# A GDN layer's head work, issued at other steps of TensorE's order

## The chip, the cores and the metric

The kernel runs on one core of a Trainium2 chip. The metric is the device time of one execution in microseconds (us); lower is better. Five engines work from queues of their own: TensorE (PE; its weight loads are shown as PEld), VectorE (DVE), ScalarE (ACT), GpSimd (POOL) and SyncE (SP), which issues the transfers.

## The reference

A trunk of two layers over one sequence of 1024 positions with 1024 channels: a gated DeltaNet (GDN) layer and an mLSTM layer, each with a residual, and a last RMS norm. Only places in the GDN layer move. For each of its 8 heads (128 key channels, 256 value channels) it computes

```python
q, k, v = split(silu(causal_dwconv(h @ w_in)))          # per head; q and k are normalised
L    = exp(gc[i] - gc[j]) for j <= i, else 0              # decay inside a chunk
a    = I + strict_lower(beta * (k @ k.T) * L)             # per chunk
u    = solve(a, beta * v)                                 # unit lower triangular
wk   = solve(a, beta * exp(gc) * k)
attn = (q @ k.T) * L
for each chunk:                                           # S: 128 x 256, carried on
    w = u - wk @ S
    o = (q * exp(gc)) @ S + attn @ w
    S = exp(gc[-1]) * S + (k * exp(gc[-1] - gc)).T @ w
out  = (rmsnorm(o) * silu(z)) @ w_out
```

The kernel works with chunks of 128 positions (8 of them, in two halves of 4) and builds the inverse of `a` for each chunk from 32x32 blocks.

## The kernel before

**The projections.** `h @ w_in` is the bulk of TensorE's work. Each operand is held as a high and a low part, and each product is three matmuls of 128x512 (high by high, high by low, low by high; the names `hh`, `hl`, `_hi`, `_lo` in line L480). One `k` of a product, three matmuls, is a *step*. The steps of all projections of the layer run one after another, head by head; a head's window is 64 steps (head 0), 96 (head 1) or 88 (heads 2 to 7); work at a step past the end stands in the next head's window.

**The head's other work** is written as Python generators, each of which issues its instructions piece by piece. A table says for each generator at which steps of its head's window it goes on by one piece: first entry head 0, second head 1, third heads 2 to 7. On TensorE the order is exactly that of the program (`manual_schedule`), so a piece's matmuls stand in TensorE's queue where the table puts them. The other engines' orders are made by a scheduler from the same program, and each engine then works through its own queue in that order, waiting at whatever isn't ready.

```python
for n, _ in enumerate(steps_of(*(c.products() for c in cols), late())):
    for gen in plan.get(n, ()):
        do(gen)
```

The generators, with the names that rows show:

- **keys** (`KEYS`, `gdn_keys`): transposes of the keys (`tpk`, L849), their squares on ACT (L852), `kd` on DVE (L873), the decay row `growb` by DMA (L858), `at` (L878), products `kk` of keys with keys (L891), from which DVE makes `nt` (L894); `nt` goes to memory and comes back as `nd` (L900, L903).
- **queries** (`QUERIES`, `gdn_queries`): transposes `tpq` (L849), their squares on ACT (`sqrq`, L852) and `eq` on DVE (L914), products `kq` (L920), which DVE multiplies into `at` (L921).
- **solve**, the substitution (`SOLVE`, `gdn_solve`): 31 pairs of DVE instructions on `nd` (`pr` L940, `xr` or `xt` L942), each pair on the result of the one before, then a way through memory (`tb_dram` L947, `td` L950).
- **merge** (`MERGE`, `gdn_merge`, once a half): DVE puts `td` into `tt` and transposes it into `t` (L959, L962, L963); TensorE makes `xp` from `t` (L971), ACT and DVE copy it to `xs` (L977, L978), TensorE makes `yp`, which is copied back into `tt` (L982 to L984); then `xl`, `xls` and `yl` in the same way at width 64.
- **values** (`TOKENS`, `gdn_tokens`): transposes of the values (L838) and their copies.
- **scan** (`SCAN`, `gdn_scan`; its table stays): per chunk `ks` from the state S (L1018), `rr` on DVE (L1020), `y` from `rr` and `tt` (L1023), `w` on ACT (L1025), `sn`, S on DVE (L1030, L1035), `o`, its RMS factor `g_r` (ACT, DVE, POOL; L392 to L394), `gv_h` on ACT (L1043), and for the chunk before the output gate `go` (L356, L359) and a store `gg_dram` (L1006).
- **blocks** (`BLOCKS`, `first_blocks`): sums and differences of input blocks (`hs`, L455 to L458, and L438) for a product scheme used from head 2 on.

The scan of a head runs while the next head's projections are on TensorE, so that scan pieces of head h and keys, solve and merge of head h+1 stand between the same projection steps. PSUM tag `d` has two banks, which `tpk`, `kk`, `tpq`, `kq`, the value transposes, the gate and the merge's products take in turn.

Of the kernel before, what the change touches and what calls it, by code (L numbers as in the profile page):

```python
# [51 lines left out]
LASTENDS = ((4, 4), (6, 8), (8, 8))  # L52


KEYS = ((4, 9, 11, 14), (28, 31, 32, 35), (22, 25, 26, 29))
QUERIES = ((17, 20, 22, 30), (68, 71, 76, 76), (82, 82, 86, 91))
SOLVE = (27, 44, 32)
MERGE = ((78, 82), (86, 93), (86, 100))
TOKENS = ((37, 37, 81, 85), (71, 74, 97, 103), (64, 68, 107, 110))
SCAN = (91, 113, 102)  # L60
PACE = ((3, 3, 8), (4, 3, 10), (4, 3, 11))
BLOCKS = (101, 115, 114, 132)
XLOADS = (24, 116)
LAST = (156, 158, 157, 159)
TH = HT * P
# [3 lines left out]
def hybrid_kernel(ctx, tc, x_in, norm_w, final_norm_w, gdn_w_in, gdn_conv_w, gdn_a_log, gdn_dt_bias, gdn_norm_w,  # L69
# [394 lines left out]
    def last_block(temp, e):  # L464

        for k in range(4):
            a = temp(k)
            whole(V, a, blocks["A12"][k])
            add_parts(V, a, a, blocks["S2"][k], ALU.subtract)
            put("S4", k, a, e)  # L470
            yield
# [358 lines left out]
    def gdn_tokens(h, st):  # L830

        for half in range(2):
            v = hp.tile([P, HT, DV], F32, tag="v", bufs=2, name=f"gv{h}_h{half}")
            st["v"].append(v)
            for e in range(ET):
                vp = pwork(f"gvp{h}_{e}_{half}", "d")
                for c in range(HT):
                    nc.tensor.transpose(vp[:, c * P:(c + 1) * P], st["vt"][e, half][:, c * P:(c + 1) * P], ident)  # L838
                A.copy(v[:, :, e * P:(e + 1) * P], vp.rearrange("p (c d) -> p c d", c=HT))
                if e == ET - 1:  # L840
                    G.tensor_tensor(v, v, st["irk"][:, half * HT:half * HT + HT].unsqueeze(2).to_broadcast([P, HT, DV]),
                                    ALU.mult)
                yield
# [62 lines left out]
    def gdn_queries(h, st):  # L906

        sq, eq = (sp.tile([P, NT], F32, tag=n, name=f"{n}{h}") for n in ("sq", "eq"))
        st["eq"] = eq
        for half in range(2):  # L910
            hs = slice(half * HT, half * HT + HT)
            q, k, at = st["q"][half], st["k"][half], st["at"][half]
            squares_t(q, sq, "q", h, half)
            V.tensor_scalar(eq[:, hs], sq[:, hs], 1e-6, EPS * DK, ALU.add, ALU.mult)  # L914
            dec_b = decay_row(1, h, half)
            yield
            kq = pwork(f"kq{h}_{half}", "d").rearrange("p (c i) -> p c i", c=HT)
            for c in range(HT):
                s_ = slice(c * P, (c + 1) * P)
                mm(kq[:, c, :], k[:, s_], q[:, s_], start=True, stop=True)  # L920
            V.tensor_tensor(at, kq, at, ALU.mult)  # L921
            G.tensor_tensor(q, q, dec_b, ALU.mult)
            yield

    def gdn_solve(h, st):


        nd = st["nd"].rearrange("p (j i) -> p j i", i=BLK)
        rows = sp.tile([P, BLK // NG4 * BLK], F32, tag="t", bufs=2, name=f"xr{h}")
        nc.sync.dma_start(rows, unit_rows)  # L930
        xp = pwork(f"xt{h}", "x")[:, :BLK // NG4 * BLK] if h > 1 else rows
        xt = xp.rearrange("p (i r) -> p i r", r=BLK)
        if h > 1:
            A.copy(xp, rows)
        yield
        for j in range(BLK - 1):
            m, n = j // NG4 + 1, BLK - 1 - j
            pr = sp.tile([P, m, n], F32, tag="td", bufs=1, name=f"pr{h}_{j}")
            with behind() if j == 0 else nullcontext():
                V.tensor_tensor(pr, xt[:, :m, j:j + 1].to_broadcast([P, m, n]),  # L940
                                nd[:, j:j + 1, j + 1:].to_broadcast([P, m, n]), ALU.mult)
            st["solved"] = V.tensor_tensor(xt[:, :m, j + 1:], xt[:, :m, j + 1:], pr, ALU.add)  # L942
            yield
        st["tb"] = dp.tile([NG4, NT, NB, BLK // NG4, BLK], F32, tag="tb", bufs=2, name=f"tb_dram{h}")
        if h > 1:
            A.copy(rows, xp)
        nc.sync.dma_start(st["tb"].rearrange("g c b i r -> (g c b) (i r)"), rows)  # L947
        st["td"] = tds = sp.tile([P, NT, BLK], F32, tag="td", bufs=1, name=f"td{h}")
        for g in range(NG4):
            nc.sync.dma_start(tds[g::NG4], st["tb"][g].rearrange("c b i r -> (b i) c r"))  # L950
        yield
# [118 lines left out]
    with tc.manual_schedule(engines={mybir.EngineType.PE}):  # L1070
# [26 lines left out]
        def at_steps(steps, gen):  # L1097
            for step in steps:
                plan.setdefault(step, []).append(gen)
# [15 lines left out]
        for h, (st, base) in enumerate(zip(sts, starts)):  # L1115
            i = min(h, 2)
            off = lambda steps: [base + n for n in steps]
            for half in range(2):
                at_steps(off(range(MERGE[i][half] - 4, MERGE[i][half] + 16, 4)), gdn_merge(h, st, half))
            at_steps(off(KEYS[i]), gdn_keys(h, st, range(2)))  # L1120
            at_steps(off(QUERIES[i]), gdn_queries(h, st))
            at_steps(off(SOLVE[i] + n // 2 for n in range(BLK + 1)), gdn_solve(h, st))
            at_steps(off(TOKENS[i]), gdn_tokens(h, st))
        temps = lambda k: [wp.tile([P, TH], F32, tag="wraw", bufs=WB, name=f"hs{k}_{i}") for i in range(2)]

        def first_blocks():
            gen = h_blocks(temps, (G, V, G))
            for k in range(4):
                with tc.issue_after(sts[0]["merged" if k else "solved"].ins):
                    next(gen)  # L1130
                yield

        at_steps(BLOCKS, first_blocks())
        at_steps(LAST, last_block(lambda k: temps(k)[0], V))
# [491 lines left out]
```

## Time and profile before

| what | value |
|---|---|
| median of 3 runs | 1971.52 us (1967.94 to 1972.74) |
| the profiled execution | 1967.29 us, its span 1965.6 us |
| TensorE busy | 1886.7 us, 96% of the span |
| DVE, ACT, POOL busy | 1271.1, 1006.8, 692.7 us |
| mean granted clock of TensorE | 0.993 |

The span is what the trace covers; the rest of the execution lies around it. A granted clock of 1.00 is TensorE at its full clock of 2.4 GHz and 0.50 at its lower level of 1.2 GHz; a number in between is a stretch with both. A row of the timeline gives start, duration, engine, line, operation, result and operands, and in brackets the time that the engine stood idle just before, with what it waited for.

### The profile page before, as it was taken

How to read it: one execution, taken by the hardware profiler on the slowest of the kernel's cores; microseconds unless marked ns; L12 is line 12 of the kernel's file. 1: busy time of each engine (PE TensorE's matmuls, PEld its weight loads, DVE VectorE, ACT ScalarE, POOL GpSimd, SP SyncE). 2: the span in 40 equal slices, each digit the busy share in tenths (PEclk: the TensorE clock that was granted, in tenths of full speed). 3: DMA queues.
4: the chain of work that ended last, by engine and by line, in shares of the span. 5: the costliest groups of instructions: out<-in, count | busy, mean ns of one | idle time of the engine just before them, and what ended most of it. 6: DMA issues, size and time to landing. Idle time of an engine off the chain costs nothing.

```text
span 1965.6 us, 28818 instructions
## 1 busy us (share of the span) xinstructions
PE 1886.7 (96%) x9768; PEld 1550.2 (79%) x9768; DVE 1271.1 (65%) x2877; ACT 1006.8 (51%) x2325; POOL 692.7 (35%) x621
## 2 busy tenths in 40 slices
PE   5998999999999999999999999999999999999987
PEld 3786787878787878787888788888888888878876
DVE  6678686858595959547555866666666666673313
ACT  5536454646465555545445554545554645564423
POOL 4234334333333334100121333333433333355553
PEclk9999999999999999999999999999999999999999
DMA  4211122121222222636421221212121221246332
GB/s 141 87 42 49 54 71 78 58 75 57 79 63 67 65 67 77 197 109 232 122 86 56 78 74 59 73 57 82 61 80 63 70 68 65 81 137 205 105 119 76
DMA packets 138620, 171.24 MB, mean 87 GB/s; under 512 B 30860, under 2 KB 68584, under 8 KB 138472
## 3 DMA queue, kind: packets, MB, share of 16 engines
q1 hardware_dynamic: 138472, 169.40, 27.5%
q8 instruction: 77, 1.26, 0.3%
q14 instruction: 71, 0.58, 0.1%
HBM read 142.87 MB, written 26.48 MB: 86 GB/s over the span
## 4 chain that ended last, share of the span: by engine, by line
PE 77%; DVE 10%; DMA 4%; ACT 3%; issue 2%; POOL 1%; SPq 1%; DVEq 0%; ACTq 0%; POOLq 0%
PE lout L679 8%; PE gkv_ps L480 7%; PE gout L679 7%; PE mkq_ps L480 7%; PE mv_ps L480 7%; PE mz_ps L480 6%; PE mog_ps L480 6%; PE gqv_ps L480 5%; PE gzp_ps L480 4%; PE mo L1455 1%; PE mv_ps L1212 1%; PE gv_ps L480 1%; PE o L1040 1%; PE y L1023 1%; PE out L384 1%
## 5 line engine op out<-in xcount | busy, mean ns | idle before, releaser
L394 POOL TENSOR_TENSOR g_r<-g_r,mhalf 128x1 f32<-128x1 f32 x64 | 41.4, 647 | 212.5 <-DVE g_r L393 192.4
L268 DVE SCALAR_TENSOR_TENSOR gw_lo<-gw_raw,rest,gw_hi 128x256 fp32r<-128x256 f32 x128 | 61.3, 516 | 66.0 <-ACT gw_hi L267 66.0
L263 POOL TENSOR_TENSOR lw_lo<-lw_raw,lw_hi 128x512 fp32r<-128x512 f32 x56 | 72.9, 1304 | 73.4 <-ACT lw_hi L262 69.9
L679 PE MATMUL lout<-lgp_hh,lw_hi 128*128 128x512 f32 x224 | 88.7, 396 | 4.6 <-DVE y L1414 3.2
L263 POOL TENSOR_TENSOR mog_lo<-mog_raw,mog_hi 128x512 fp32r<-128x512 f32 x39 | 50.3, 1290 | 115.3 <-ACT mog_hi L262 115.3
L263 POOL TENSOR_TENSOR mz_lo<-mz_raw,mz_hi 128x512 fp32r<-128x512 f32 x39 | 53.8, 1379 | 99.7 <-ACT mz_hi L262 99.7
L267 ACT ACTIVATE gw_hi<-gw_raw,rest 128x256 fp32r<-128x256 f32 x128 | 58.0, 501 | 58.3 <-PE gout L679 42.3
L679 PE MATMUL lout<-lgp_hl,lw_hi 128*128 128x512 f32 x224 | 87.7, 392 | 0.0
L679 PE MATMUL lout<-lgp_hh,lw_lo 128*128 128x512 f32 x224 | 86.8, 392 | 0.0
L263 POOL TENSOR_TENSOR mv_lo<-mv_raw,mv_hi 128x512 fp32r<-128x512 f32 x38 | 51.4, 1353 | 84.1 <-ACT mv_hi L262 53.1
L263 POOL TENSOR_TENSOR gkv_lo<-gkv_raw,gkv_hi 128x512 fp32r<-128x512 f32 x40 | 52.8, 1322 | 78.3 <-ACT gkv_hi L262 67.8
L480 PE MATMUL gkv_ps<-hh,gkv_hi 128*128 128x512 f32 x176 | 78.9, 448 | 0.0
L263 POOL TENSOR_TENSOR gzp_lo<-gzp_raw,gzp_hi 128x512 fp32r<-128x512 f32 x38 | 49.7, 1307 | 66.8 <-ACT gzp_hi L262 55.4
L262 ACT CAST lw_hi<-lw_raw 128x512 fp32r<-128x512 f32 x56 | 34.7, 620 | 73.7 <-PE lout L679 48.9
L263 POOL TENSOR_TENSOR mkq_lo<-mkq_raw,mkq_hi 128x512 fp32r<-128x512 f32 x35 | 45.6, 1302 | 75.9 <-ACT mkq_hi L262 64.8
L480 PE MATMUL gkv_ps<-hh,gkv_lo 128*128 128x512 f32 x176 | 69.2, 393 | 0.0
L480 PE MATMUL gkv_ps<-hl,gkv_hi 128*128 128x512 f32 x176 | 69.0, 392 | 0.0
L679 PE MATMUL gout<-glp_hh,gw_hi 128*128 128x512 f32 x160 | 66.7, 417 | 0.0
L394 POOL TENSOR_TENSOR m_r<-m_r,mhalf 128x1 f32<-128x1 f32 x64 | 42.6, 665 | 66.2 <-DVE m_r L393 65.2
L679 PE MATMUL gout<-glp_hl,gw_hi 128*128 128x512 f32 x160 | 62.7, 392 | 0.0
L679 PE MATMUL gout<-glp_hh,gw_lo 128*128 128x512 f32 x160 | 62.7, 392 | 0.0
L1043 ACT ACTIVATE gv_h<-o,g_r 128x256 f32<-128x256 f32 x64 | 30.3, 473 | 62.5 <-POOL g_r L394 61.8
(769 smaller groups left out, 6688.0 us busy)
## 6 DMA issues: line engine op xcount, KB each, us to landing
gw_raw<-in_gdn_w_out_dram SPq DMA_DIRECT2D x64, 256.0 KB, 2.7
lw_raw<-in_mlstm_w_out_dram SPq DMA_DIRECT2D x56, 256.0 KB, 2.7
gzp_raw<-in_gdn_w_in_dram SPq DMA_DIRECT2D x32, 256.0 KB, 3.2
growb<-g_dram SPq DMA_DIRECT2D x32, 256.0 KB, 3.2
gg_dram<-gv_h SPq DMA_DIRECT2D x64, 128.0 KB, 1.8
gl<-gg_dram SPq DMA_DIRECT2D x32, 256.0 KB, 3.4
mog_raw<-in_mlstm_w_in_dram SPq DMA_DIRECT2D x32, 256.0 KB, 3.1
mz_raw<-in_mlstm_w_in_dram SPq DMA_DIRECT2D x32, 256.0 KB, 2.9
```

The costliest lines, as they stand in the source:

```text
L262: A.copy(hi, raw)
L263: (e or G).tensor_tensor(lo, raw, hi.bitcast(F32), ALU.subtract)
L267: A.activation(hi[:, k], raw[:, k], AF.Copy, scale=c)
L268: V.scalar_tensor_tensor(lo[:, k], raw[:, k], c, hi.bitcast(F32)[:, k], ALU.mult, ALU.subtract)
L384: mm(ps, a[:, e, ds], b[:, e, hs], start=m == 0, stop=m == 3 * ET - 1)
L394: G.tensor_tensor(r, r, mhalf[:, :1], ALU.pow)
L480: mm(ps, w_[:, k, :], h_, start=first and k == 0 and i == 0, stop=k == 3 and i == 2, skip_group_check=True)
L679: mm(pss[2 * j + i], a[:, e, i * P:(i + 1) * P], b, start=h == heads[0] and e == 0 and m == 0, stop=h == heads[-1] and e == ET - 1 and m == 2)
L1023: mm(yp[:, :DV], st["tt"][half][:, cc, :], rr, start=True, stop=True)
L1040: mm(op[:, :DV], st["at"][half][:, cc, :], w, start=S is None, stop=True)
L1043: A.activation(v, op[:, :DV], AF.Copy, scale=r)
L1212: mm(ps[c], h_[k][half][:, c * P:(c + 1) * P], w_[:, k % 2, :], start=k == 0 and i == 0, stop=k == KT - 1 and i == 2)
```

## The change

Places in the tables move; no instruction is added or taken away, and no shape changes.

```diff
-KEYS = ((4, 9, 11, 14), (28, 31, 32, 35), (22, 25, 26, 29))
-QUERIES = ((17, 20, 22, 30), (68, 71, 76, 76), (82, 82, 86, 91))
-SOLVE = (27, 44, 32)
-MERGE = ((78, 82), (86, 93), (86, 100))
-TOKENS = ((37, 37, 81, 85), (71, 74, 97, 103), (64, 68, 107, 110))
+KEYS = ((2, 7, 8, 15), (32, 35, 36, 39), (22, 25, 26, 29))
+QUERIES = ((17, 20, 23, 30), (68, 71, 76, 76), (80, 80, 84, 89))
+SOLVE = (24, 44, 32)
+MERGE = ((78, 82), (86, 89), (88, 100))
+TOKENS = ((37, 37, 81, 85), (71, 74, 97, 103), (64, 74, 107, 110))
...
-BLOCKS = (101, 115, 114, 132)
+BLOCKS = (101, 115, 114, 126)
```

Head 0's keys and substitution go up to three steps earlier, head 1's keys four steps later, head 1's second merge half four steps earlier, and the blocks' last piece six steps earlier. For heads 2 to 7 (one table entry, so the same places six times) the queries go two steps earlier, the first half of the merge two steps later and the second piece of the values six steps later. What that makes of the queues is shown at three places.

TensorE's queue in the late part of head 5's window. `hh_6_1` is the activation of k = 6, second half of the positions; `xp_0`, `yp_0` are the merge of head 5, first half; `tpq_1`, `kq_1` its queries, second half; `ks_7`, `y_7` the scan of head 4, last chunk; `gzp` and `gkv` are projections. Before:

```order
L480 MATMUL gzp_ps_6232<-hh_6_1_435,gzp_4_lo 128x512
L971 MATMUL xp_0_6342<-t_0_6278,nt_0_5652 32x32 x8
L849 MATMUL tpq_1_6354<-ident,gqT_1_6091 128x128 x4
L480 MATMUL gzp_ps_6232<-hh_7_1_440,gzp_4_hi 128x512
...
L1018 MATMUL ks_7_6372<-S_6_6313,gkT_1_4472 128x256
L480 MATMUL gkv_ps_6376<-hh_0_0_233,gkv_00_hi 128x512
...
L971 MATMUL yp_0_6392<-xs_0_6351,tt_0_6277 32x32
...
L1023 MATMUL y_7_6411<-rr_7_6374,tt_1_5434 128x256
L920 MATMUL kq_1_6415<-gqT_1_6091,gkT_1_5500 128x128 x4
```

And after:

```order
L849 MATMUL tpq_1_6336<-ident,gqT_1_6091 128x128 x4
...
L480 MATMUL gzp_ps_6232<-hh_7_1_440,gzp_4_lo 128x512
L1018 MATMUL ks_7_6360<-S_6_6308,gkT_1_4472 128x256
L480 MATMUL gkv_ps_6364<-hh_0_0_233,gkv_00_hi 128x512
...
L971 MATMUL xp_0_6374<-t_0_6332,nt_0_5652 32x32 x8
...
L920 MATMUL kq_1_6389<-gqT_1_6091,gkT_1_5500 128x128 x4
...
L1023 MATMUL y_7_6402<-rr_7_6362,tt_1_5434 128x256
...
L971 MATMUL yp_0_6409<-xs_0_6383,tt_0_6331 32x32
```

`xp_0` has moved behind `tpq_1`, the three matmuls of k = 7, `ks_7` and the next product's first three matmuls; `kq_1` now stands ahead of `y_7`, and `yp_0` behind it.

DVE's queue at the same place (`t_0`, `xs_0`, `tt_0` belong to the merge, `rr_7` to the scan, `eq` to the queries, `gzp_u` and `gkv_raw` to the projections). Before:

```order
L962 STREAM_TRANSPOSE t_0_6278<-tt_0_6277 64x256
L525 TENSOR_TENSOR gkv_raw_6028<-gkv_raw_6028,gkv_raw_6025 128x512
L978 COPY xs_0_6351<-xp_0_6342 32x128
L614 TENSOR_TENSOR gzp_u_6098<-gzp_u_6098,gzp_ps_6232 128x512
L1020 SCALAR_TENSOR_TENSOR rr_7_6374<-ks_7_6372,nlam,gv_h_5554 128x256
L963 STREAM_TRANSPOSE t_1_6463<-td_5992 32x4x32
L914 TENSOR_SCALAR eq_6283<-sq_6282 128x4
L983 COPY tt_0_6277<-yp_0_6392 32x4x32
```

And after:

```order
L962 STREAM_TRANSPOSE t_0_6332<-tt_0_6331 64x256
L525 TENSOR_TENSOR gkv_raw_6028<-gkv_raw_6028,gkv_raw_6025 128x512
L914 TENSOR_SCALAR eq_6272<-sq_6271 128x4
L614 TENSOR_TENSOR gzp_u_6098<-gzp_u_6098,gzp_ps_6232 128x512
L1020 SCALAR_TENSOR_TENSOR rr_7_6362<-ks_7_6360,nlam,gv_h_5554 128x256
L963 STREAM_TRANSPOSE t_1_6463<-td_5992 32x4x32
L978 COPY xs_0_6383<-xp_0_6374 32x128
L921 TENSOR_TENSOR at_1_5682<-kq_1_6389,at_1_5682 128x512
```

The copy `xs_0` has gone behind `rr_7`, and `eq` ahead of it.

SP's queue in head 1's window (`growb` the decay rows, `nt_dram` and `nd` the way of the keys' `nt` through memory, `gg_dram` the scan's store, `gzp_raw` and `gkv_raw` loads of weights). Before:

```order
L490 DMA gzp_raw_1283<-in_gdn_w_in_dram 128x512 x2
L858 DMA growb_0_2003<-g_dram 128x512
L900 DMA nt_dram_0_1498<-nt_0_1493 32x4x32 x4
L903 DMA nd_1428<-nt_dram_0_1498 16x1024 x4
L900 DMA nt_dram_1_1567<-nt_1_1562 32x4x32 x4
L1006 DMA gg_dram<-gv_h_1027 128x2x128
L903 DMA nd_1428<-nt_dram_1_1567 16x1024 x4
L490 DMA gkv_raw_1718<-in_gdn_w_in_dram 128x512 x2
```

And after:

```order
L490 DMA gzp_raw_1283<-in_gdn_w_in_dram 128x512 x2
L858 DMA growb_1_1547<-g_dram 128x512
L858 DMA growb_0_2020<-g_dram 128x512
L900 DMA nt_dram_0_1524<-nt_0_1519 32x4x32 x4
L1006 DMA gg_dram<-gv_h_1045 128x2x128
L903 DMA nd_1475<-nt_dram_0_1524 16x1024 x4
L490 DMA gkv_raw_1718<-in_gdn_w_in_dram 128x512
L900 DMA nt_dram_1_1614<-nt_1_1609 32x4x32 x4
L490 DMA gkv_raw_1718<-in_gdn_w_in_dram 128x512
L903 DMA nd_1475<-nt_dram_1_1614 16x1024 x4
```

The transfers of `nt` to memory and of `nd` back now stand between the store and two loads of weights, and a load stands ahead of each of the last two.

On TensorE head 1's keys stand like this: `tpk_0`, `kk_0`, `tpk_1` and `kk_1` were behind the first-chunk scan's `sn_0` (ahead of it for `tpk_0`), `o_0`, `ks_1` and `y_1`; now `tpk_0` is behind `ks_1`, `kk_0` behind `y_1`, `tpk_1` three matmuls after it, and `kk_1` behind `go_0`. In head 0, `tpk_0` now stands right behind `gr_ps` (L783), ahead of six projection matmuls that stood between.

## Rows read from the trace of the kernel before

**Rows 1.** The page's first part: engine, busy us, share of the span, instructions.

```profile
PE 1886.7 (96%) x9768; PEld 1550.2 (79%) x9768; DVE 1271.1 (65%) x2877; ACT 1006.8 (51%) x2325; POOL 692.7 (35%) x621
```

**Rows 2.** TensorE's waits: what waited, for what, total us, times, longest us.

```profile
PE xp L971 <- DVE t L962: 12.7, 6, 2.6
...
PE kk L891 <- DVE nt L894: 4.1, 1, 4.1
...
PE y L1023 <- DVE xr L942: 2.1, 1, 2.1
```

**Rows 3.** Timeline: merge's first products, heads 3, 4, 5, 7.

```profile
414.50 0.64 PE L971 MATMUL xp<-t,nt 32*32 32x32 f32 x16 [2.60 <-DVE t L962]
...
510.20 0.44 PE L971 MATMUL xp<-t,nt 32*32 32x32 f32 x16 [2.21 <-DVE t L962]
...
603.83 0.44 PE L971 MATMUL xp<-t,nt 32*32 32x32 f32 x16 [1.56 <-DVE t L962]
...
792.35 0.44 PE L971 MATMUL xp<-t,nt 32*32 32x32 f32 x16 [2.52 <-DVE t L962]
```

**Rows 4.** Timeline, TensorE behind head 5's `xp_0`.

```profile
604.20 0.66 PE L849 MATMUL tpq<-ident,gqT 128*128 128x128 f32 x4
...
605.65 0.58 PE L480 MATMUL gkv_ps<-hh,gkv_hi 128*128 128x512 f32 x1
...
606.54 0.40 PE L480 MATMUL gkv_ps<-hh,gkv_hi 128*128 128x512 f32 x1
...
609.18 0.59 PE L1023 MATMUL y<-rr,tt 128*128 128x256 f32 x2
609.61 1.05 PE L920 MATMUL kq<-gqT,gkT 128*128 128x128 f32 x8
```

**Rows 5.** Timeline, DVE at the same place.

```profile
601.79 0.69 DVE L959 TENSOR_TENSOR tt<-td,dmask 128x512 f32<-128x512 f32 x1 [1.42 <-DMA td<-tb_dram]
...
603.25 0.43 DVE L962 STREAM_TRANSPOSE t<-tt 64x256 f32<-64x256 f32 x1
...
605.81 0.69 DVE L614 TENSOR_TENSOR gzp_u<-gzp_u,gzp_ps 128x512 f32<-128x512 f32 x1
606.42 0.48 DVE L1020 SCALAR_TENSOR_TENSOR rr<-ks,nlam,gv_h 128x256 f32<-128x256 f32 x1
...
607.45 0.70 DVE L914 TENSOR_SCALAR eq<-sq 128x4 f32<-128x4 f32 x1 [0.23 <-ACT sqrq L852]
```

**Rows 6.** Timeline, ACT at the same place.

```profile
604.70 0.47 ACT L1043 ACTIVATE gv_h<-o,g_r 128x256 f32<-128x256 f32 x1 [3.72 <-POOL g_r L394]
...
606.14 0.61 ACT L262 CAST gkv_hi<-gkv_raw 128x512 fp32r<-128x512 f32 x1
```

**Rows 7.** Stretches: us, busy of PE, PEld, DVE, ACT, POOL, granted clock, DMA share, GB/s.

```profile
158.00:168.00 10.00, 6.44 (x27) 5.64 (x28) 9.62 (x24) 6.21 (x14) 5.57 (x4) 0.83 0.35 96
...
412.00:420.00 8.00, 5.50 (x34) 4.47 (x34) 4.26 (x11) 2.72 (x11) 2.54 (x2) 0.79 0.13 37
508.00:514.00 6.00, 3.80 (x33) 3.29 (x34) 4.27 (x11) 2.61 (x11) 2.05 (x2) 1.00 0.23 64
```

**Rows 8.** Timeline, TensorE behind `xp_0` of heads 3 and 7.

```profile
417.67 0.59 PE L480 MATMUL gkv_ps<-hh,gkv_hi 128*128 128x512 f32 x1
...
795.14 0.99 PE L679 MATMUL gout<-glp_hh,gw_hi 128*128 128x512 f32 x1
...
796.65 0.39 PE L679 MATMUL gout<-glp_hh,gw_hi 128*128 128x512 f32 x1
```

**Rows 9.** Timeline, DVE in head 1's window.

```profile
173.04 0.69 DVE L458 TENSOR_TENSOR hs<-hs,x 128x512 f32<-128x512 f32 x1 [1.70 <-POOL S1hl L438]
```

**Rows 10.** Timeline, DVE in head 0's window.

```profile
72.45 0.28 DVE L785 COPY gr_sb<-gr_ps 64x128 f32<-64x128 f32 x1 [0.39 <-PE gr_ps L783]
```

**Rows 11.** Timeline, DVE late in head 1's window.

```profile
213.91 0.17 DVE L914 TENSOR_SCALAR eq<-sq 128x4 f32<-128x4 f32 x1 [1.90 <-ACT sqrq L852]
```

**Rows 12.** SP's waits from 150 to 200 us, columns as in rows 2.

```profile
SPq L490 <- POOL gvq_lo L263: 15.0, 1, 15.0
```

## The prediction, made before the change was timed

> **What bounds the kernel now.** I read the page's busy times first: TensorE is busy for 96% of the span, no other engine for more than 65% [rows 1]. So the time is TensorE's work plus what TensorE waits, and a change of order can win only waits and the clock that they cost. Next its waits [rows 2]. The largest that the tables can touch is `xp`, the first products of the merge: 12.7 us in six waits on the transpose `t`, one in each of heads 2 to 7. Then two waits in head 1's window: 4.1 us of `kk_1` on `nt`, and 2.1 us of `y_3`, put down to the solve's `xr`, that is, to DVE being late. Third, the timeline around one `xp_0` [rows 3 to 6] and the granted clock around four of the waits [rows 7, 8].
>
> At head 5 the reader is to see who is late: DVE's `tt` waits 1.42 us for `td` to come back from memory, `t_0` starts at 603.25 and is done at 603.68, and `xp_0` starts at 603.83 after 1.56 us of standing [rows 3, 5]. TensorE has work that needs nothing of the merge, but it stands behind `xp_0` in its queue.
>
> **Heads 2 to 7, the merge two steps on.** Ahead of `xp_0` now stand `tpq_1`, three matmuls, `ks_7` and three more, which before stood behind it. Their length is read where they run at full clock: from 604.20 to 606.54, 2.34 us [rows 4]. None waits for the merge, so the time at which `t_0` is ready stays and `xp_0` comes 2.34 us later in the queue. The six waits are 2.60, 2.21, 1.56 and 2.52 [rows 3] and two that make up the 12.7. Only 2.60 and 2.52 are longer than the cover: 0.26 and 0.18 stay, and 12.2 go. Bounds: nothing if `t_0` moves back by as much as TensorE comes forward; all 12.7.
>
> **The clock behind the waits.** After the 2.60 the granted clock of 412 to 420 us is 0.79, so part of it ran at 1.2 GHz; after the 2.21 that of 508 to 514 is 1.00 [rows 3, 7]. What the slow stretch costs is read from the same eight instructions. Head 3: from 414.50 to 417.67, 3.17 us; head 5: 603.83 to 605.65, 1.82 [rows 3, 4, 8]. That is 1.35 lost. Head 7: 792.35 to 795.14 is 2.79, 0.97 lost, and the next three matmuls and a little, 795.14 to 796.65, take 1.51 against 0.89 (605.65 to 606.54), 0.62 lost [rows 3, 4, 8]. Together 2.9. With waits of 0.26 and 0.18 in place of 2.60 and 2.52 I take all of it. Bounds: 0 and 2.9.
>
> The Trainium skill, TensorE: Matmul & The Clock Gate, section "HAM oscillation — how this bites in real kernels", says that a wait long enough throttles the array, and that the work behind it starts at the lower clock. The rows agree for 2.60 and 2.52 and show no such loss behind 2.21. By the rule the 2.9 return in full; by a reading in which the drop belongs to the place and not the wait, none does, and the time is 2.9 higher.
>
> **What is late next in these heads: `y_7`.** TensorE comes forward, DVE doesn't, so `rr_7` has less lead over `y_7`. Before, `rr_7` was done at 606.90 and `y_7` began at 609.18, 2.28 later [rows 4, 5]. Now `y_7` is wanted earlier by the wait that goes (1.56 to 2.34), and later by part of `kq_1`, which comes ahead of it (1.05) while `yp_0` goes behind; I take 0.4 for the two. So it is wanted at 608.0 at head 5 and at 607.2 where 2.34 go. But on DVE `rr_7` now stands behind `eq`, and `eq` behind ACT's squares, which stand behind `gv_h`, done at 605.17 [rows 6]. In the trace `eq` starts at 607.45, with a weight cast of 0.61 among the squares on ACT [rows 5, 6]; in ACT's order now the cast stands behind them. Without it `eq` could start at 606.84; then 0.17 for `eq` as in [rows 11], 0.61 for `gzp_u` (605.81 to 606.42) and 0.48 for `rr_7` [rows 5] make 608.1. ACT's copy of `xs`, which stood ahead of the squares, now comes behind, so a little less: 607.7. That is nothing at head 5, and up to 0.5 where 2.34 go. I take −1.2 for the six heads. Bounds: 0, and −7.2 (rival B).
>
> The merge's half 0 as a whole ends two steps later. Its last products `yl_0` now stand two steps ahead of `y_0` of the same head, by the tables, with ACT's copy between; a step is 0.7 to 0.9 us (0.89 in [rows 4]) and an ACT instruction of 256 columns 0.47 [rows 6]: 0, and if ACT is late by one such instruction, −0.3 a head, −1.8 in all. `kq_1` and its `at` come earlier and feed the same scan: 0. The values' second piece goes six steps later; its copies run on ACT and POOL, busy for 51% and 35% [rows 1], and are read in the scan: 0.
>
> **Head 1.** Its keys go four steps later and `kk_1` from behind `y_1` to behind `go_0`, so that its wait on `nt` (4.1) should nearly go. But DVE there is full: 9.62 of 10 us between 158 and 168 [rows 7]. What TensorE no longer waits at `kk_1` it will wait for DVE further on, at `y_3` or at a state update, unless DVE itself comes forward, and it can do that only by its idle time. The largest piece of that which the moved keys can touch is the 1.70 ahead of `hs` at 173.04 [rows 9], just before the solve's first product and `rr_3`. I take that, +1.7. Bounds: −1.7 (as much again is added, since at the other end the solve starts later) and 6.2 + 1.7 (both waits go, and the granted clock of 0.83 in those 10 us comes back [rows 2, 7]).
>
> **Head 1's second merge half**, four steps earlier: the trace gives TensorE little wait in that stage, and DVE's next free place may put it at either side: 0, bounds ±0.9. **Blocks**, six steps earlier: work that runs on DVE and POOL, with two heads until it is read: 0.
>
> **Head 0.** `tpk_0` stands right behind `gr_ps` and takes a bank that `gr_sb` must leave on DVE. That copy starts at 72.45 after 0.39 of waiting and takes 0.28 [rows 10], so `tpk_0` waits about 0.5: −0.5, bounds −1.5 (a clock that stays low a little longer) and 0. The substitution three steps earlier: 0, it is far ahead of its readers.
>
> **The sum.** 12.2 + 2.9 − 1.2 + 1.7 − 0.5 = 15.1. The profiled execution took 1967.3, so 1952.2 by its own measure. It lies 4.2 below the median of the runs shown, 1971.5; put against that median, the time is **1956.4**.
>
> **The rivals.**
>
> *B: DVE's order gives half of it back.* For it: `eq` in the trace really starts at 607.45 and takes 0.70 there [rows 5]. If that holds, `gzp_u` and `rr_7` end at 609.2, and `y_7`, wanted at 608.0, waits 1.2 in each head, 7.2 in all; head 1 gives nothing, since its DVE is full, and half the clock's 2.9 comes back. 12.2 − 7.2 + 1.5 − 0.5 = 6.0: 1965.5. Against it: ACT's queue without the cast and `xs`. Its row: DVE does let a state update wait behind an `eq` that isn't ready, 1.90 us in [rows 11]. The Trainium skill, Perfetto Trace Analysis, section "Tensor Engine Instruction (MATMUL, LD_WEIGHTS)", states it as a rule, that these engines work strictly in order; it speaks against this change, and the trace agrees.
>
> *C: nothing is won.* `t_0` hangs on the solve, the solve on DVE, and DVE takes its pace from TensorE's products between the pairs. If TensorE's 2.34 us come out of the same chain, `xp_0` waits as before: 12.2 and 2.9 fall away, 1.7 − 0.5 stay or not, and the time is 1970 to 1971.5. Against it: `tt` waits for a transfer there [rows 5], and what has moved ahead of `xp_0` feeds neither.
>
> *D: slower.* In head 1 the loads of `nd` stand behind loads of weights on SP, and such a load has held SP for 15.0 us in this stage, waiting for its buffer [rows 12]. If one holds the second `nd`, the solve's first product holds DVE's queue, `rr_3` is late and TensorE stands 15.0, and 1.6 more at the lower clock (as in head 7). The rest of the sum, 12.2 + 2.9 − 1.2 − 0.5 = 13.4, doesn't cover it: +3.2, 1974.7; two such holds, one for each `nd`, make 1990. It decides from 13.4 − 1.6 = 11.8 us of standing on. Against it: the buffers of those loads are freed by products that TensorE has done by then.
>
> **How the numbers follow.** Forecast 0.67, its own range 1949 to 1962 (from 22 us won: both waits and clock of head 1, to 9: head 1 at −1.7 and `y_7` at half of B); B 0.16; C 0.10; D 0.07. Within 0.3% (5.9 us) a measurement of this kernel can't be told from no change; the bound is 1965.6. Faster by more: nearly all of the forecast, and over half of B, since 1965.5 sits on the bound: 0.76. Slower by more: two holds of D, or a cover that I took for granted: 0.06. Within: the rest, 0.18. The range that leaves out two in ten takes in B and leaves out C, D and a rest below: 1949 to 1967.
>
> **What would show it.** Right: `xp` on `t` falls from 12.7 to under 1 in TensorE's waits; the clock of the stretches behind `xp_0` in heads 3 and 7 is 1.00; `y` on `rr` appears with about 0.2 a head; `kk_1` waits under 1, `y_3` or a row near it still 1 to 3. Wrong: six waits of over 1 us at `y_7` (B); six at `xp_0` as now (C); a load on SP that waits over 10 us ahead of an `nd` (D).

## The result, and the profile after

Six runs of the changed kernel have a median of 1958.92 us (1954.93 to 1961.26), six of the kernel before 1971.81 (1967.94 to 1975.57). The ratio is 0.9937, 95% interval 0.9922 to 0.9952: 12.9 us faster (the prediction said 15.1, and a time of 1956.4). In a second series the ratio was 0.9918 (0.9901 to 0.9934), 17.9 us between the medians. The profiled execution after took 1959.62 us, its span 1957.9.

The first view is that of TensorE's waits after, with the columns of [rows 2]; the lines of projections, gates and the mLSTM layer, which are much as before, and some of 0.2 us are left out. A number behind a name (`xp_1`) is the half of the positions, or for the scan the chunk.

```profile
PE tpk L849 <- DVE kd L873: 4.5, 2, 3.5
...
PE y L1023 <- DVE rr L1020: 2.1, 1, 2.1
...
PE kk L891 <- DVE tt L992: 1.8, 5, 0.4
PE yp L971 <- DVE tt L984: 1.6, 1, 1.6
...
PE kk L891 <- DVE kd L873: 0.9, 1, 0.9
PE tpk L849 <- DVE gr_sb L785: 0.4, 1, 0.4
...
PE yp L971 <- DVE xs L978: 0.3, 1, 0.3
```

The line `xp` on `t`, 12.7 us, is gone, and no `y` waits in heads 2 to 7. The 2.1 at `y` and most of the 4.5 at `tpk` stand in head 1, as does the new 1.6 at `yp`.

Where the time went is read by the start of each projection's first matmul in the two timelines. The difference changes only where one of them waits or runs at a lower clock:

| from the first matmul of ... | before | after | after − before |
|---|---|---|---|
| `gv`, head 0 | 67.00 | 66.81 | −0.2 |
| `gzp`, head 0 | 99.39 | 99.49 | +0.1 |
| `gzp`, head 1 | 195.19 | 195.90 | +0.7 |
| `gkv`, head 2 | 231.57 | 235.52 | +4.0 |
| `gqv`, head 2 | 265.12 | 270.30 | +5.2 |
| `gqv`, head 6 | 643.73 | 638.56 | −5.2 |
| `gout` (end of head 7) | 795.14 | 784.19 | −11.0 |
| the first `mkq` of the mLSTM layer | 1110.49 | 1100.65 | −9.8 |
| span | 1965.6 | 1957.9 | −7.7 |

Heads 2 to 7 win 16.1 us (from +5.2 to −11.0), head 1 loses 5.1 of it again, head 0 0.3. The rest is in code that didn't change: 1.1 in the mLSTM layer up to that first `mkq` and 2.1 behind it, over half of that from 1862 us on, where the granted clock differs (0.58 from 1862 to 1873 after, 0.69 for the same stretch before, 1871 to 1882; 0.72 and 0.79 in the last 21 us).

At head 5, the place of [rows 3 to 6], the timeline after shows on TensorE, DVE and ACT:

```profile
599.96 0.59 PE L1018 MATMUL ks<-S,gkT 128*128 128x256 f32 x2
...
601.18 0.44 PE L971 MATMUL xp<-t,nt 32*32 32x32 f32 x16
...
602.36 1.05 PE L920 MATMUL kq<-gqT,gkT 128*128 128x128 f32 x8
...
604.63 0.59 PE L1023 MATMUL y<-rr,tt 128*128 128x256 f32 x2
```

```profile
598.52 0.43 DVE L962 STREAM_TRANSPOSE t<-tt 64x256 f32<-64x256 f32 x1
...
601.13 0.17 DVE L914 TENSOR_SCALAR eq<-sq 128x4 f32<-128x4 f32 x1 [1.61 <-ACT sqrq L852]
...
601.81 0.48 DVE L1020 SCALAR_TENSOR_TENSOR rr<-ks,nlam,gv_h 128x256 f32<-128x256 f32 x1
```

```profile
598.52 0.28 ACT L852 ACTIVATE sqrq<-tpq 128x128 bf16<-128x128 f32 x1
...
599.97 0.47 ACT L1043 ACTIVATE gv_h<-o,g_r 128x256 f32<-128x256 f32 x1 [1.07 <-POOL g_r L394]
600.34 0.27 ACT L852 ACTIVATE sqrq<-tpq 128x128 bf16<-128x128 f32 x1
```

`t` is ready at 598.95, 2.2 us ahead of `xp`: more than the 0.8 that a cover of 2.34 against a wait of 1.56 leaves. So the chain to `t` has come forward by some 1.4 us as well. SP's queue shows most of it. Before, the solve's result went out behind a load of weights, and `td` followed 3.07 us later:

```profile
593.57 0.80 SPq L490 DMA_DIRECT2D gqv_raw<-in_gdn_w_in_dram  x2
594.46 0.38 SPq L947 DMA_DIRECT2D tb_dram<-xr  x1
597.53 2.56 SPq L950 DMA_DIRECT2D td<-tb_dram  x4
```

After, it goes first, and `td` follows 1.77 us later:

```profile
590.42 0.33 SPq L947 DMA_DIRECT2D tb_dram<-xr  x1
590.84 0.88 SPq L490 DMA_DIRECT2D gqv_raw<-in_gdn_w_in_dram  x2
592.19 2.56 SPq L950 DMA_DIRECT2D td<-tb_dram  x4
```

It is the same in heads 3 and 6 (3.3 and 3.1 us before, 1.8 after). In heads 2 and 4, where no load stood just ahead, the time falls by 0.7 and 0.2; in head 7 it grows from 2.4 to 2.9, and `t` is done there only 0.15 us before `xp` starts, as it was where `xp` waited: in head 7 nothing of the margin is left.

In head 1's merge TensorE now waits twice within 2 us:

```profile
229.69 0.44 PE L356 MATMUL go_gp<-ident,gv_h 128*128 128x128 f32 x2 [0.37 <-DVE xs L978]
231.71 0.18 PE L971 MATMUL yp<-xs,tt 32*32 32x32 f32 x1 [1.57 <-DVE tt L984]
```

and of the stretches from there (columns of [rows 7]) the middle two run at or near the lower level, 1.2 GHz, though TensorE is busy:

```profile
228.00:232.00 4.00, 2.05 (x32) 1.28 (x30) 3.88 (x8) 2.09 (x4) 0.16 (x1) 1.00 0.02 4
232.00:236.00 4.00, 4.00 (x30) 2.99 (x21) 1.18 (x4) 1.86 (x5) 0.00 (x0) 0.61 0.21 66
236.00:240.00 4.00, 4.00 (x19) 2.94 (x18) 0.00 (x0) 0.94 (x2) 1.28 (x1) 0.54 0.00 0
240.00:244.00 4.00, 4.00 (x28) 2.87 (x28) 0.00 (x0) 0.95 (x2) 0.00 (x0) 1.00 0.02 4
```

That is 4 × 0.39 + 4 × 0.46 = 3.4 us of lost clock behind 1.9 us of waiting.

### The profile page after: what moved, and what is told of

Same layout as the page of the kernel before. It is cut to its first block, busy times and chain, and to the rows that moved or that the text cites. A ratio compares the mean times of both kernels' runs of the same rounds, so it can differ in the third digit from the quotient of the medians.

```text
span 1957.9 us, 28802 instructions
## 1 busy us (share of the span) xinstructions
PE 1891.6 (97%) x9768; PEld 1552.7 (79%) x9768; DVE 1271.2 (65%) x2877; ACT 1010.5 (52%) x2325; POOL 691.2 (35%) x621
## 4 chain that ended last, share of the span: by engine, by line
PE 86%; DVE 5%; ACT 3%; DMA 2%; issue 1%; POOL 0%; SPq 0%; DVEq 0%; ACTq 0%; POOLq 0%
PE gout L679 9%; PE gzp_ps L480 8%; PE lout L679 8%; PE gkv_ps L480 7%; PE mkq_ps L480 7%; PE mv_ps L480 7%; PE mz_ps L480 7%; PE gqv_ps L480 6%; PE mog_ps L480 6%; PE o L1040 1%; PE mo L1455 1%; PE y L1023 1%; PE mv_ps L1212 1%; PE sn L1030 1%; PE o L1039 1%; PE ks L1018 1%
## 5 line engine op out<-in xcount | busy, mean ns | idle before, releaser
L263 POOL TENSOR_TENSOR gqv_lo<-gqv_raw,gqv_hi 128x512 fp32r<-128x512 f32 x30 | 38.8, 1293 | 64.8 <-PE sn L1030 25.2
```

The source lines that it names most:

```text
L263: (e or G).tensor_tensor(lo, raw, hi.bitcast(F32), ALU.subtract)
```

## The experiments

Each was timed in up to five rounds beside the kernel before on the same chip; the ratios are to that. There are three series of four kernels. "Head 2's queries" is the start of their projection, `gqv` in the table above; late and early are against the profile of the kernel before.

**Heads 2 to 7 alone**

```diff
 (before)
-QUERIES = (..., (82, 82, 86, 91))    MERGE = (..., (86, 100))    TOKENS = (..., (64, 68, 107, 110))
+QUERIES = (..., (80, 80, 84, 89))    MERGE = (..., (88, 100))    TOKENS = (..., (64, 74, 107, 110))
```

> Only the third entries of MERGE, QUERIES and TOKENS are as after (heads 2 to 7); heads 0 and 1 and the blocks stay as before. Theory: heads 2 to 7 alone win more than the whole change, because head 1 costs about 5 us in the changed kernel: from the start of head 2's query projection to head 7's end the two traces differ by 16.1 us. So this kernel should be 15 to 16.5 us faster than before (ratio 0.9917 to 0.9924), and head 2's queries should start at 265 us as before, not at 270. Rival: the moved keys of head 1 free DVE for the later heads, and the gain of heads 2 to 7 hangs on it; then it is no faster than the changed kernel, 11 to 13 us (0.9934 to 0.9944).

Measured: 1952.80 us, ratio 0.9893 (0.9881 to 0.9906), 21 us faster. In its timeline head 2's queries start 0.3 late and `gout` 15.6 early: 15.9. The theory holds against its rival; its number was too small, since the median wins 5 us more than the trace (see the clock, below).

**Merge half of head 1 back**

```diff
 (after)
-MERGE = ((78, 82), (86, 89), (88, 100))
+MERGE = ((78, 82), (86, 93), (88, 100))
```

> The changed kernel with head 1's second merge half at its old step (93), all else as after. Theory: this one entry costs about 4.5 us in the changed kernel (head 1's end slips from +0.7 to +5.2 us: a wait of 1.57 us at yp and then a stretch at the lower clock); so it should be 4 to 5 us faster than the changed kernel, 16 to 17 faster than before (ratio 0.9914 to 0.9920), with no granted clock under 0.95 between 228 and 245 us. Rival: the later keys of head 1 make DVE late there, whatever the merge's place; then the wait and the lower clock stay, and the ratio is that of the changed kernel, 0.9937.

Measured: 0.9901 (0.9888 to 0.9915), 1954.66. By the ratio the theory could stand, by the trace it falls: TensorE still waits in head 1's merge, now 1.39 us at `xp_1`, the clock behind is 0.68 (230 to 236 us), and head 2's queries start 5.0 late, 1.4 of it from head 0. The wait is there whatever the merge's place, as the rival says, but the rival's ratio, 0.9937, lies outside the interval.

**Merge half of head 1 alone**

```diff
 (before)
-MERGE = ((78, 82), (86, 93), (86, 100))
+MERGE = ((78, 82), (86, 89), (86, 100))
```

> The kernel before with head 1's second merge half at step 89 in place of 93, nothing else. Theory: it costs 4 to 5 us by itself (ratio 1.0020 to 1.0025), with a wait of 1 to 2 us at yp near 230 us and the lower clock behind it. Rival (keys are what makes DVE late there): 0 to 1 us, ratio 1.0000 to 1.0005, and no lower clock.

Measured: 0.9998 (0.9986 to 1.0010). `yp` waits 1.01 us, nothing is lost behind it. The rival holds: this entry by itself costs nothing that shows.

**Merge of heads 2 to 7 alone**

```diff
 (before)
-MERGE = ((78, 82), (86, 93), (86, 100))
+MERGE = ((78, 82), (86, 93), (88, 100))
```

> The kernel before with the first merge half of heads 2 to 7 at step 88 in place of 86, nothing else (queries and values stay). Theory: the merge's place alone is the gain, since tpq, ks and six projection matmuls come ahead of xp by it alone: 15 to 16.5 us faster than before, ratio 0.9917 to 0.9924, xp's waits on t under 1 us in all. Rival: the earlier queries are needed, since kq then stands between xp and yp and covers the copy of xs; without it yp waits 0.5 to 1 us a head, and the gain is 10 to 13 us (0.9934 to 0.9950).

> The kernel with the merge of heads 2 to 7 alone moved, once more, so that the three others stand beside it on one chip. Theory: ratio 0.988 to 0.991 as in its first series. If it were over 0.992, the first series would have flattered it, and the changed kernel's other edits would cost nothing.

Measured: 1952.41, 0.9897 (0.9882 to 0.9912), and again 0.9897 (0.9872 to 0.9923). That is 21 us, more than the theory's 15 to 16.5. So one number of the table makes all of the gain that can be measured. The waits of `xp` from 300 to 800 us in the first trace:

```profile
PE xp L971 <- DVE t L962: 0.8, 2, 0.4
```

In the two traces `xp` waits twice, 0.43 and 0.40, then 0.49 and 0.31; in the other heads `t` is ready 0.2 to 1.4 us ahead, against 1.5 to 2.2 in heads 2 to 6 where queries and values are moved too. In heads 3, 5 and 6 SP has the weight load ahead of `tb_dram` here, as before. So the queries and values buy margin, with SP's order, but no time that can be measured.

**The changed kernel again, and with head 1 and head 0's keys as before**

```diff
 (after; the second of the two)
-KEYS = ((2, 7, 8, 15), (32, 35, 36, 39), ...)    MERGE = (..., (86, 89), ...)
+KEYS = ((4, 9, 11, 14), (28, 31, 32, 35), ...)   MERGE = (..., (86, 93), ...)
```

> The changed kernel itself once more, beside the next two on one chip, since the earlier kernels were timed in another series. Theory: head 1's moved keys cost it about 5 us against the same kernel with head 1 as before (of that under 1 us of waits, the rest TensorE's lower clock behind a wait at head 1's merge), so it stands at a ratio of 0.992 to 0.995, 4 to 8 us above the kernel in which head 1 is as before. Rival: what sets it apart from the kernel with heads 2 to 7 alone was the series, and it is now within 2 us of that.

> The changed kernel with all of head 1 and the keys of head 0 as before (heads 2 to 7 as after; head 0's queries and solve and the blocks as after). Theory: it loses nothing of what heads 2 to 7 win: 0.9885 to 0.9905, 19 to 22 us faster than before and 4 to 8 faster than the changed kernel. Rival: blocks or the solve of head 0 carry the cost; then it stays with the changed kernel at 0.992 to 0.995.

Measured: 1956.35, 0.9918 (0.9901 to 0.9934), against 1953.46, 0.9895 (0.9879 to 0.9911). The medians are 2.9 us apart, less than the theory's 4 to 8 and more than the rival's 2, and the intervals overlap. In the traces head 1 loses 2.4 (after again; 5.1 the first time) and nothing. The size of the loss goes with the clock behind the wait: 0.73 and 0.98 from 230 to 236 and 236 to 242 us here, 0.74 and 0.69 the first time, after the same wait of 1.57. A single trace says little of it: in the second trace of the kernel with the merge of heads 2 to 7 alone, head 1 loses 3.2 though nothing there was touched, by the clock behind its old waits (0.66 and 0.83 in 160 to 170 and 180 to 190 us, against 0.83 and 1.00 in the first). So what is shown is the wait in the merge; that it makes the median 2.9 longer is likely, not shown.

**Keys of head 1 alone**

```diff
 (before)
-KEYS = ((4, 9, 11, 14), (28, 31, 32, 35), (22, 25, 26, 29))
+KEYS = ((4, 9, 11, 14), (32, 35, 36, 39), (22, 25, 26, 29))
```

> The kernel before with head 1's keys at steps 32, 35, 36, 39 in place of 28, 31, 32, 35, nothing else. Theory: the keys make DVE late in head 1's merge, so this edit alone costs: 0.5 to 1 us of waits by the start of head 1's gate product and 3 to 4.5 us more by head 2's queries where the clock falls: 2 to 6 us slower than before, ratio 1.001 to 1.003. Rival: the cost comes from keys and merge half together; then it is 0 to 1 us and head 2's queries start within 1 us of before.

Measured: 0.9990 (0.9979 to 1.0001). The wait at `kk_1` becomes one of 3.6 at `tpk_1`, the one at `y` becomes two of 1.2 and 1.0, and head 1 loses 0.1. The theory falls: the keys alone cost nothing that shows.

**Keys of head 1 back, blocks back**

```diff
 (after)
-KEYS = (..., (32, 35, 36, 39), ...)       (the second kernel:)  -BLOCKS = (101, 115, 114, 126)
+KEYS = (..., (28, 31, 32, 35), ...)                             +BLOCKS = (101, 115, 114, 132)
```

> The changed kernel with only head 1's keys as before (its second merge half stays at 89, the blocks at 126). Theory: the later keys are needed for the loss in head 1, since they put DVE behind there; with the keys back yp waits 1.0 us as in the kernel with the merge half alone, the clock stays at 1.00 behind it, and head 2's queries start within 1.5 us of before; ratio 0.989 to 0.991. Rival: the merge half with the earlier block is enough; then the lower clock stays, head 2's queries start 3 to 5 us late, ratio 0.9915 to 0.993.

> The changed kernel with only the blocks' last piece back at step 132 (keys and merge half of head 1 stay moved). The kernel with the keys alone moved, blocks at 132, had no wait over 0.6 us in head 1's merge; the two with keys moved and blocks at 126 had 1.4 to 1.6 us and the lower clock. Theory: late keys and the early block together make DVE 2 us late; with the block back no wait in head 1's merge is over 0.7 us and the clock is 1.00 from 228 to 245 us; head 2's queries start 1 to 2.5 us late, ratio 0.989 to 0.991. Rival: keys and merge half together are enough: a wait over 1 us and the lower clock stay, ratio 0.9915 to 0.993.

Measured: 0.9894 (0.9868 to 0.9920) and 0.9905 (0.9878 to 0.9931), two intervals that don't tell the theories from the rivals; the traces do. With the keys back `yp` waits 0.91, the clock stays at 1.00, and head 2's queries start 0.3 late. With the blocks back the wait is the old one:

```profile
230.54 0.18 PE L971 MATMUL yp<-xs,tt 32*32 32x32 f32 x1 [1.57 <-DVE tt L984]
...
230.00:236.00 6.00, 5.46 (x44) 4.04 (x44) 1.97 (x6) 2.44 (x5) 1.28 (x1) 0.72 0.17 44
```

So the theory on the keys holds and that on the blocks falls. In the changed kernel the late keys are needed for the wait in the merge to reach 1.4 to 1.6 and for the clock to fall there: without them the merge half leaves waits of 0.91 and 1.01 and a clock of 1.00. By themselves they don't make it (0.52 at `xp_1`, clock 1.00). Which edit makes it with them where the merge half is back was not found; and the last kernel below comes to 1.41 at `xp_1` with one piece of head 1's keys moved and no other edit in head 1.

**The merge of heads 2 to 7 the other way**

```diff
 (before)
-MERGE = ((78, 82), (86, 93), (86, 100))
+MERGE = ((78, 82), (86, 93), (84, 100))
```

> The kernel before with the first merge half of heads 2 to 7 at step 84 in place of 86, the other way from the change. Six matmuls fewer stand ahead of xp, 1.36 us at full clock. Theory: t isn't ready any earlier, so each of the six waits grows by 1.3 to 1.4 us to 2.9 to 4.0, 8.2 us in all, and a wait of that length drops the clock in all six heads, 1.3 to 1.6 us each, of which the kernel before pays two in its trace: 8 to 14 us slower, ratio 1.004 to 1.007, granted clock under 0.9 behind xp in five or six heads. Rival 1: t comes earlier with the order (DVE's queue follows TensorE's): waits as before, ratio within 1.001. Rival 2: the lower clock belongs to heads 3 and 7 as places: 8.2 us, 1.0042, and clock 1.00 behind xp in heads 2, 4, 5 and 6.

Measured: 1.0068 (1.0054 to 1.0082), 13 us slower.

```profile
PE xp L971 <- DVE t L962: 22.1, 6, 4.0
```

The six waits are 3.3 to 4.0 each, together 9.4 more than before, and the clock behind five of the six is 0.66 to 0.82. The theory holds: `t` doesn't come earlier with TensorE's order, and the clock is paid in heads 2, 4 and 5 too.

**Two more places of keys**

```diff
 (merge of heads 2 to 7 alone)
-KEYS = ((4, 9, 11, 14), (28, 31, 32, 35), (22, 25, 26, 29))
+KEYS = ((4, 9, 11, 14), (28, 31, 32, 37), (22, 26, 26, 29))
```

> Aimed at a version that beats both: heads 2 to 7's first merge half at 88 as the only part of the change, and two places of keys that the change left: head 1's kk_1 two steps later (its last entry 37 for 35) and kk_0 of heads 2 to 7 one step later (26 for 25). Theory: six projection matmuls now cover 1.4 of the 4.1 us that kk_1 waits in head 1, and the clock there may stay up, and the five waits of kk_0 (0.35 to 0.6 us) go: 2 to 5 us faster than the kernel with the merge alone, ratio 0.9875 to 0.989. Rival: DVE is full in head 1, so what kk_1 doesn't wait comes back at y_3 or at a state update; then 1 to 2 us, 0.989 to 0.990.

Measured: 1959.32, 0.9916 (0.9893 to 0.9938), 3.4 us above the median of the kernel with the merge alone in the same series. The theory's 0.9875 to 0.989 lies outside the interval, and there is no gain; whether it is slower is not shown, since the intervals overlap. The wait at `kk_1` falls from 4.1 to 2.75, but `y_3` still waits 2.2, `xp_1` of head 1's merge 1.4, and the clock behind that falls to 0.81. The five waits of `kk_0` went to `tpk_1` behind it, 0.26 to 0.47 each.

Put beside each other, the kernels with heads 2 to 7's merge at 88 fall into two groups. With head 1's keys at their old places the five ratios are 0.9893 to 0.9897; with all or one of these keys later the five (the last kernel above, which moves a key piece of heads 2 to 7 as well, among them) are 0.9901 to 0.9937. Pairs of them overlap, but the grouping speaks for a cost of the late keys of some 1 to 8 us.

## Why the prediction was right, and which steps failed

**The merge, 12.2.** Right: all 12.7 went, and the same table entry moved the other way added 9.4 us of these waits. That `t` doesn't move back when TensorE comes forward was right; that SP's order would bring it forward was missed, to the good (the sum left 0.4 of the waits standing, so no more than that was in it).

**The clock, 2.9.** Right in the trace: behind `xp` of heads 3 and 7 the profile after has

```profile
417.00:425.00 8.00, 8.00 (x77) 6.26 (x76) 4.14 (x10) 2.08 (x8) 2.58 (x2) 1.00 0.09 33
785.00:793.00 8.00, 7.50 (x73) 5.68 (x72) 6.17 (x14) 5.19 (x13) 1.97 (x2) 1.00 0.52 172
```

(The stretch that the price is read from holds six rows, not eight instructions; its times are read rightly.) But the step that took the profiled execution for the kernel failed, and it is the largest error that the total hides. Adding 4.2 to come from the trace to the median treats them as time that stays. In the timed runs of before in the first series the mean granted clock is 0.984 to 0.989, in the profiled one 0.993; and other kernels with these waits show the drop in other heads. With the keys alone moved, behind waits of 2.10 and 1.65 us:

```profile
321.77 0.41 PE L971 MATMUL xp<-t,nt 32*32 32x32 f32 x15 [2.10 <-DVE t L962]
...
605.58 0.44 PE L971 MATMUL xp<-t,nt 32*32 32x32 f32 x16 [1.65 <-DVE t L962]
...
322.00:330.00 8.00, 8.00 (x76) 6.74 (x71) 5.28 (x11) 3.60 (x15) 2.92 (x3) 1.00 0.07 19
...
606.00:614.00 8.00, 8.00 (x57) 6.48 (x57) 3.79 (x10) 3.35 (x13) 1.69 (x2) 0.79 0.06 17
```

Two of six waits drop the clock in the profile of before, four of six in that of the keys alone and in that of the merge half alone, none where the merge stands at 88. So heads 2 to 7 are worth 20 to 21 us of the median (the kernels with them alone) and 15 to 16 of the trace. By the prediction's own measure, profiled execution against profiled execution, the changed kernel is 7.7 us faster the first time and 14.9 the second (1959.62 and 1952.36 against 1967.29): one kernel, nearly the same waits, another clock.

**`y_7`, −1.2.** Failed, to the good: 0. `rr` ends at 602.29 and `y` starts at 604.63, a lead of 2.3 as before. The step had all four squares behind `gv_h` on ACT. With `tpq_1` two steps earlier two of them run ahead of it, `eq` starts 1.16 behind `gv_h` and takes 0.17, and the chain in front has come forward too. In the two kernels with the queries unmoved `y_7` doesn't wait either; there `kq_1` of head 7 waits 0.6 for the squares.

**Head 1, +1.7.** Failed, with the wrong sign: −5.1 in the first trace, −2.4 in the second, −2.9 between the medians of one series (likely, not shown). That TensorE can win there only what DVE can give was right: the waits by head 2's first keys sum to 9.15 before and 9.62 after. The bound of −1.7 was the mistake. It priced only DVE's next idle time. What the late keys cost appears in the merge 50 us on, where TensorE waits 1.4 to 1.6 us for DVE and ACT, and the clock behind that costs up to 3.4 more; with the keys back the wait is 0.91 and the clock 1.00.

**Head 0, −0.5.** Right: `tpk` waits 0.38, and 0.3 are lost. (Two of head 0's places, the last of its keys and the third of its queries, go one step later, which the section on the change doesn't say; in the first trace nothing waits there, in the second `kq` 0.56 us.)

**Merge half of head 1, blocks, values, solve: 0.** The merge half alone costs nothing (0.9998), the queries and values of heads 2 to 7 neither win nor lose (0.9893 with them, 0.9897 without), the blocks were only put back in the changed kernel, and the solve was not run apart. That the merge half meets the late keys was not weighed.

**Rivals.** B fell with `y_7`, C with `xp`. D: SP issues the second `nd` at 175.01 against 169.33, and no load from the first `nt_dram` to it waits for a buffer (the one that waits, 12.0 us, is issued at 153.30, ahead of both halves).

So the two main terms were right in mechanism; that the total came so near is luck, for two errors offset: 6 to 7 us too little for heads 2 to 7 by the median (13.9 for 20 to 21), and some 5 too much for head 1 (+1.7 for −2.9). The measured parts add up to some 17.5, which is the second series' 17.9; the first series' 12.9 is 5 less, and what makes the two differ is not shown. The changed kernel is not the best that was run: the one with heads 2 to 7's merge at 88 alone, or with queries and values beside it, has the lower ratio (0.9897 and 0.9893 against 0.9937 and 0.9918).

## What to carry to other kernels

Where an engine runs one fixed order, a wait with independent work behind it goes by putting that work ahead, and the margin is read from the trace as the length of what moves past. A wait that TensorE has where another engine is full was only shifted here by TensorE's order: price it by what that engine does later, up to its next meeting with TensorE. And a profiled execution is one draw: where short waits may or may not drop the clock, compare its granted clock with that of the timed runs before its terms are put against the median.

## What the runs showed of the hardware that was not expected

The clock behind a wait is not settled by the wait's length between about 1.4 and 3.3 us: 2.10 us at the same place in head 2 left it at 1.00 in two kernels (before, and head 1's keys alone) and dropped it to 0.79 in a third, that with the merge half of head 1 alone:

```profile
319.50 0.44 PE L971 MATMUL xp<-t,nt 32*32 32x32 f32 x16 [2.10 <-DVE t L962]
...
320.00:328.00 8.00, 8.00 (x56) 6.46 (x57) 4.61 (x10) 3.54 (x15) 1.81 (x2) 0.79 0.02 7
```

With head 1's keys alone moved 1.58 dropped it in head 6, and with the merge the other way 3.26 left it at 1.00 in head 6 for the 8 us behind it. The Trainium skill, TensorE: Matmul & The Clock Gate, section "HAM oscillation — how this bites in real kernels", tells that a long wait throttles the array. The waits of 3.3 to 4.0 us agree in five heads of six; the shorter ones did it in some executions and not in others. The price where it fell was 1.35 and 1.6 us in heads 3 and 7 of before and up to 3.4 us in head 1's merge.
